# Row sums of a 64 MiB array: three row blocks of 32, 48 and 48 in place of two of 80 and 48, and the early stores issued one load earlier

## The chip, the core and the metric

The kernel runs on one core of a Trainium2 chip. Its time is the device time of one execution in microseconds (us). The kernel before was run three times: 160.71, 161.05 and 161.06 us, so its median is 161.05 us. One further execution was taken with the profiler; it took 160.77 us, of which the trace covers a span of 159.4 us.

## The reference: what is computed

The input `x` is float32 of shape 32 x 512 x 1024. The output is the sum over the last axis, float32 of shape 32 x 512:

```python
def reference(x):
    return np.sum(x, axis=-1).astype(np.float32)
```

Seen flat, that is 16384 rows of 1024 numbers (4 KiB each), 67.1 MB to read, and 16384 sums (64 KiB) to write. There are two float32 numbers of reading for each addition, so the work is almost only the reading.

## The kernel before, in words

**Layout.** The 128 partitions of the on-chip memory share the 16384 rows, 128 rows to each. Rows are dealt out in two blocks. Block a holds the first 128 x 80 rows: partition p gets 80 neighbouring rows, so where partition p+1 starts lies 80 rows (320 KiB) after partition p in the chip's main memory. Block z holds the other 128 x 48 rows in the same manner, with 48 rows (192 KiB) from one partition to the next. This distance is called the pitch below. The output of a block is cut likewise: partition p writes 80, or 48, neighbouring sums.

**Loads.** A block is read in groups of 16 rows a partition (G), so that one full load moves 128 x 64 KiB = 8.39 MB. Block a makes five groups (b = 0 to 4) and block z two (b = 5, 6); the last 16 rows of block z are read in smaller pieces of 9, 4 and 2 rows (`CUTS`: piece0, piece1, piece2) and the very last row in two parts of 544 and 480 numbers (tail0, tail1). Group 0 is read as one row (`first`) and 15 rows. Groups rotate through three buffers xt0 to xt2 (BUFS). All DMAs are issued by SyncE (SP in the profile), in the order of the list `loads` (line 134). From the fourth group on each load first waits until VectorE has finished the group that used the buffer before (line 133). The first two loads are moved ahead of the start barrier (lines 158 to 177).

**Sums.** VectorE sums each group with one reduction (lines 56 to 63) into `res_a` or `res_z`. In group 6 it takes 9 rows and ScalarE the other 7, one activation with accumulation for each (lines 65 to 71). The pieces are shared out in the same manner (lines 113 to 123); the two parts of the last row are summed by VectorE with a fused add and reduction (lines 73 to 79, called in lines 125 and 128), the second of which yields the last sum.

**Stores.** Behind all loads, SP waits for tail0's landing (line 135), for VectorE and ScalarE to have finished groups 0 to 6 (lines 136 and 137), and then issues two early stores: the 80 sums a partition of block a and the first 32 of block z (lines 138 and 139). Then it waits for all of VectorE's and ScalarE's work (lines 140 and 141) and issues the last store, 16 sums a partition (line 142). At the end it waits for both early stores and clears the semaphores (lines 145 and 146), and waits for the last store (line 147).

The order of instructions is written out by hand: each engine runs its own list in program order, and waits are on semaphores. A DMA adds 16 to its semaphore when it has landed, one for each of the 16 DMA engines that carry it.

Of the kernel before, what the change touches and what calls it, by code (L numbers as in the profile page):

```python
# [6 lines left out]
COPY = mybir.ActivationFunctionType.Copy  # L7
X = mybir.AxisListType.X

BODY = 80  # L10
Z = 48
G = 16
BUFS = 3
ACT_ROWS = 7
# [5 lines left out]
def row_sums(nc, x: bass.AP, out: bass.AP):  # L20
    P = nc.NUM_PARTITIONS
    x_flat = x.flatten_outer_dims()
    R, D = x_flat.shape
    C = R // P
    assert R % P == 0 and C == BODY + Z and BODY % G == 0 and Z % G == 0
    out_flat = out.rearrange("a (b c) -> (a b c)", c=1)

    def block(r0, n):
        x_b = x_flat[r0 : r0 + P * n].rearrange("(p c) d -> p (c d)", p=P)
        out_b = out_flat[r0 : r0 + P * n].rearrange("(p c) -> p c", p=P)  # L30
        return x_b, out_b

    x_a, out_a = block(0, BODY)
    x_z, out_z = block(P * BODY, Z)

    def sbuf(name, n):
        return nc.alloc_sbuf_tensor(name, [P, n], F32)

    xt = [sbuf(f"xt{i}", G * D) for i in range(BUFS)]
    tail = sbuf("tail", D + 16)  # L40
    pairs = [sbuf(f"pairs{i}", D // 2) for i in range(3)]
    res_a = sbuf("res_a", BODY)
    res_z = sbuf("res_z", Z)
    z0 = Z - G

    names = [f"slot{i}" for i in range(BUFS)] + ["first", "piece0", "piece1", "piece2", "tail0"]
    names += ["tail1", "vec", "act", "early_store", "store"]
    sems = {n: nc.alloc_semaphore(n) for n in names}
    slots = [sems[f"slot{i}"] for i in range(BUFS)]
    vec, act = sems["vec"], sems["act"]  # L50
    numbers = [s.num for s in sems.values()]
    assert numbers == list(range(numbers[0], numbers[0] + len(numbers)))

    count = {"vec": 0, "act": 0}

    def rows_dve(t, j, n, res, c):
        nc.vector.tensor_reduce(  # L57
            out=res[:, c : c + n],
            in_=t[:, j * D : (j + n) * D].rearrange("p (j d) -> p j d", d=D),
            axis=X,  # L60
            op=ADD,
        ).then_inc(vec, 1)
        count["vec"] += 1

    def rows_act(t, j, n, res, c):
        for i in range(n):
            v = t[:, (j + i) * D : (j + i + 1) * D]
            nc.scalar.activation(  # L68
                out=v, in_=v, func=COPY, accum_out=res[:, c + i : c + i + 1]
            ).then_inc(act, 1)  # L70
            count["act"] += 1

    def pairs_dve(t, a, b, acc, pairs):
        h = (a + b) // 2
        nc.vector.tensor_tensor_reduce(  # L75
            out=pairs[:, 0 : h - a], in0=t[:, a:h], in1=t[:, h:b], scale=1.0, scalar=0.0,
            op0=ADD, op1=ADD, accum_out=acc,
        ).then_inc(vec, 1)
        count["vec"] += 1

    n_bufs = (C - G) // G


    freed = {}
    loads = []
    for b in range(n_bufs):
        x_b, c = (x_a, b * G) if b * G < BODY else (x_z, b * G - BODY)
        parts = [(0, G, slots[b % BUFS])] if b else [(0, 1, sems["first"]), (1, G, slots[0])]
        for i, j, s in parts:
            loads.append((b, xt[b % BUFS][:, i * D : j * D], x_b[:, (c + i) * D : (c + j) * D], s))  # L90
    last = xt[n_bufs % BUFS]
    for k, (i, j) in enumerate(zip(CUTS, CUTS[1:])):
        loads.append((n_bufs, last[:, i * D : j * D], x_z[:, (z0 + i) * D : (z0 + j) * D], sems[f"piece{k}"]))
    for k, (i, j, gap) in enumerate(((0, CUT, 0), (CUT, D, 16))):
        e = (Z - 1) * D
        loads.append((0, tail[:, i + gap : j + gap], x_z[:, e + i : e + j], sems[f"tail{k}"]))


    nc.vector.memset(tail[:, CUT + 15 : CUT + 16], 0.0).then_inc(vec, 1)  # L99
    count["vec"] += 1  # L100
    nc.vector.wait_ge(sems["first"], 16)
    for b in range(n_bufs):
        a = ACT_ROWS if b == n_bufs - 1 else 0
        nc.vector.wait_ge(slots[b % BUFS], 16 * (b // BUFS + 1))
        res, c = (res_a, b * G) if b * G < BODY else (res_z, b * G - BODY)
        rows_dve(xt[b % BUFS], 0, G - a, res, c)
        freed[b] = count["vec"]
        if a:
            nc.scalar.wait_ge(slots[b % BUFS], 16 * (b // BUFS + 1))
            rows_act(xt[b % BUFS], G - a, a, res, c + G - a)  # L110
    body_vec, body_act = count["vec"], count["act"]

    for k in range(2):
        i, j = CUTS[k], CUTS[k + 1]
        h = (j - i) // 2
        nc.vector.wait_ge(sems[f"piece{k}"], 16)
        rows_dve(last, i, h, res_z, z0 + i)
        nc.scalar.wait_ge(sems[f"piece{k}"], 16)
        rows_act(last, i + h, j - i - h, res_z, z0 + i + h)
    nc.scalar.wait_ge(sems["piece2"], 16)  # L120
    rows_act(last, 14, 1, res_z, z0 + 14)
    nc.vector.wait_ge(sems["piece2"], 16)
    pairs_dve(last, 13 * D, 14 * D, res_z[:, z0 + 13 : z0 + 14], pairs[2])
    nc.vector.wait_ge(sems["tail0"], 16)
    pairs_dve(tail, 0, CUT, tail[:, CUT + 14 : CUT + 15], pairs[0])
    nc.vector.wait_ge(sems["tail1"], 16)
    nc.vector.wait_ge(vec, count["vec"])
    pairs_dve(tail, CUT + 14, D + 16, res_z[:, Z - 1 : Z], pairs[1])


    for b, dst, src, s in loads:
        if b >= BUFS:
            nc.sync.wait_ge(vec, freed[b - BUFS])
        nc.sync.dma_start(out=dst, in_=src).then_inc(s, 16)  # L134
    nc.sync.wait_ge(sems["tail0"], 16)
    nc.sync.wait_ge(vec, body_vec)
    nc.sync.wait_ge(act, body_act)
    nc.sync.dma_start(out=out_a, in_=res_a[:, :]).then_inc(sems["early_store"], 16)
    nc.sync.dma_start(out=out_z[:, 0:z0], in_=res_z[:, 0:z0]).then_inc(sems["early_store"], 16)
    nc.sync.wait_ge(vec, count["vec"])  # L140
    nc.sync.wait_ge(act, count["act"])
    nc.sync.dma_start(out=out_z[:, z0:Z], in_=res_z[:, z0:Z]).then_inc(sems["store"], 16)


    nc.sync.wait_ge(sems["early_store"], 32)
    nc.sync.sem_clear(range(numbers[0], sems["store"].num))
    nc.sync.wait_ge(sems["store"], 16).then_inc(sems["store"], -16)


def kernel(tc: tile.TileContext, x: bass.AP, out: bass.AP):  # L150
    tc.close()
    tc.compile()  # L152
    nc = tc.nc
    row_sums(nc, x, out)

    sp = mybir.EngineType.SP
    fn = nc.m.functions[0]
    entry, body = None, None  # L160
    for blk in fn.blocks:
        ops = [i for i in blk.instructions if i.engine == sp]
        if entry is None:
            entry = blk
        elif any(i.opcode == "DMACopy" for i in ops):
            body = blk
            break
    code = list(body.instructions)
    loads = [i for i in code if i.engine == sp and i.opcode == "DMACopy"][:EARLY]
    for load in loads:  # L170
        assert not load.sync_info.on_wait
        code.remove(load)
    body.instructions = code
    code = list(entry.instructions)
    at = next(k for k, i in enumerate(code) if i.engine == sp and i.opcode == "Drain")
    code[at:at] = loads
    entry.instructions = code
# [29 lines left out]
```

## Time and profile before

| what | value |
|---|---|
| median of three runs | 161.05 us (160.71 to 161.06) |
| the profiled execution | 160.77 us |
| its traced span | 159.4 us |
| VectorE (DVE) busy | 121.4 us, 76% of the span |
| ScalarE (ACT) busy | 17.2 us, 11% |
| DMA | 98.0% of 16 engines' span, 67.18 MB, mean 421 GB/s |
| one full reduction, 16 rows | 17.22 us |
| DMA packets | 2304 |

The profile has several views. The chain of waits follows the work that ended last backwards, and prints it in order of time. The timeline lists instructions by start, with the idle time of the engine before them and what ended it. The stretches table gives each engine's busy time, the DMA share and GB/s between two times. Below all this the trace keeps a record of every DMA packet (start, duration, bytes) and of every increment of a semaphore by a landed DMA; a packet of a full load is one partition's 64 KiB. Records are counted to a stretch by their start, so a DMA share above 1 in a short stretch means that long packets started in it. "SPq" in the views is the queue of instructions of SyncE: its DMA issues count as no engine's busy time.

### The profile page before, as it was taken

Reading aid. Unit: us, or ns where it says so; the run is one execution under the profiler, and the core shown is the slowest. Engines: PE = TensorE matmul, PEld = TensorE weight load, DVE = VectorE, ACT = ScalarE, POOL = GpSimd, SP = SyncE. Lnnn points to the kernel's source line nnn. Section 1 sums busy time; section 2 is a strip of 40 time slices with the busy share of each in tenths; the row PEclk is TensorE's granted clock in tenths of the full one; section 3 lists DMA queues with packets and bytes.
Section 4 is the critical chain, followed back from the end, with each engine's and each line's share of the span. In section 5 each row is a group of like instructions: output and inputs, shape, how many; then the busy total and the mean of one; then the engine's idle time right before and its main releaser. Section 6 shows DMA issues by size and latency. Waiting matters only on the chain.

```text
span 159.4 us, 108 instructions
## 1 busy us (share of the span) xinstructions
DVE 121.4 (76%) x16; ACT 17.2 (11%) x31; POOL 0.2 (0%) x4
## 2 busy tenths in 40 slices
DVE  0000049998699968999599994999949999499785
ACT  3000000000000000000000000000000000394694
POOL 0000000000000000000000000000000000000000
DMA  9969996996997989969969969969969989699994
GB/s 378 493 293 447 493 526 263 526 493 296 526 460 329 526 378 411 526 296 493 526 263 526 526 263 526 510 280 526 493 296 526 427 362 526 296 444 444 395 405 138
DMA packets 2304, 67.18 MB, mean 421 GB/s; under 512 B 640, under 2 KB 768, under 8 KB 1024
## 3 DMA queue, kind: packets, MB, share of 16 engines
q1 hardware_dynamic: 2304, 67.18, 98.0%
HBM read 67.11 MB, written 0.07 MB: 421 GB/s over the span
## 4 chain that ended last, share of the span: by engine, by line
DMA 75%; DVE 22%; SPq 1%; issue 0%
DMA xt<-in_x_dram 50%; DMA tail<-in_x_dram 25%; DVE res_a L57 22%; SPq L134 1%; DVE pairs L75 0%; DVE res_z L75 0%
## 5 line engine op out<-in xcount | busy, mean ns | idle before, releaser
L57 DVE TENSOR_REDUCE res_a<-xt 128x16 f32<-128x16384 f32 x5 | 86.1, 17220 | 28.4 <-DMA xt<-in_x_dram 28.4
L57 DVE TENSOR_REDUCE res_z<-xt 128x16 f32<-128x16384 f32 (+3 forms) x4 | 33.7, 8420 | 5.9 <-DMA xt<-in_x_dram 5.9
L68 ACT ACTIVATE xt<-xt 128x1024 f32<-128x1024 f32 x15 | 15.6, 1043 | 138.3 <-DMA xt<-in_x_dram 138.3
L68 ACT ACTIVATION_READ_ACCUMULATOR xt<-xt 128x1 f32 x15 | 2.8, 186 | 0.0
L99 DVE MEMSET tail<- 128x1 f32 x1 | 0.1, 59 | 2.0 <-PEq L152 2.0
L68 ACT ACT_TABLE_LOAD x1 | 1.3, 1283 | 1.9 <-PEq L152 1.9
L75 DVE CUSTOM_DVE_ANT_0 pairs<-tail 128x272 f32<-128x272 f32 (+1 forms) x2 | 0.9, 427 | 0.1
L75 DVE CUSTOM_DVE_ANT_0 pairs<-xt 128x512 f32<-128x512 f32 x1 | 0.7, 693 | 0.2 <-DMA xt<-in_x_dram 0.2
L75 DVE DVE_READ_ACCUMULATOR2_ANT res_z<- 128x1 f32 x2 | 0.2, 84 | 0.0
L191 POOL MEMSET const-bfloat16-1.0<- 128x1 bf16 x1 | 0.1, 102 | 0.0
L191 POOL MEMSET const-uint8-127<- 128x1 uint8 x1 | 0.1, 102 | 0.0
L191 POOL MEMSET const-float32-1.0<- 128x1 f32 x1 | 0.1, 99 | 0.0
L191 POOL MEMSET const-float32-0.0<- 128x1 f32 x1 | 0.1, 98 | 0.2 <-issue 0.2
L75 DVE DVE_READ_ACCUMULATOR2_ANT tail<- 128x1 f32 x1 | 0.1, 83 | 0.0
## 6 DMA issues: line engine op xcount, KB each, us to landing
xt<-in_x_dram SPq DMA_DIRECT2D x1, 7680.0 KB, 21.4
xt<-in_x_dram SPq DMA_DIRECT2D x1, 4608.0 KB, 32.3
xt<-in_x_dram SPq DMA_DIRECT2D x1, 2048.0 KB, 36.9
xt<-in_x_dram SPq DMA_DIRECT2D x1, 1024.0 KB, 38.9
xt<-in_x_dram SPq DMA_DIRECT2D x1, 512.0 KB, 3.7
tail<-in_x_dram SPq DMA_DIRECT2D x1, 272.0 KB, 39.1
tail<-in_x_dram SPq DMA_DIRECT2D x1, 240.0 KB, 39.2
xt<-in_x_dram SPq DMA_DIRECT2D x6, 40.8
```

The lines of the kernel that those rows point to most:

```text
L57: nc.vector.tensor_reduce(out=res[:, c : c + n], in_=t[:, j * D : (j + n) * D].rearrange("p (j d) -> p j d", d=D), axis=X, op=ADD,).then_i ...
L68: nc.scalar.activation(out=v, in_=v, func=COPY, accum_out=res[:, c + i : c + i + 1]).then_inc(act, 1)
L75: nc.vector.tensor_tensor_reduce(out=pairs[:, 0 : h - a], in0=t[:, a:h], in1=t[:, h:b], scale=1.0, scalar=0.0, op0=ADD, op1=ADD, accum_out ...
L99: nc.vector.memset(tail[:, CUT + 15 : CUT + 16], 0.0).then_inc(vec, 1)
L134: nc.sync.dma_start(out=dst, in_=src).then_inc(s, 16)
L191: nc = _bacc.Bacc("TRN2", target_bir_lowering=False, num_devices=1)
```

## The change

Two things are changed. The rows are dealt out in three blocks of 32, 48 and 48 rows a partition. Groups, buffers, pieces and reductions keep their sizes and their order: the first block makes two groups of 16 rows, the second three, the third two and the same pieces. The pitch is 128 KiB in the first block and 192 KiB in the other two. The results of a block lie in a tensor of their own (`sums[k]`), so there are three early stores, of 32, 48 and 32 sums a partition.

The early stores' first wait is for piece2, the load ahead of tail0, and no longer for tail0; the other two waits stay. The three stores follow one another with no further wait. The wait ahead of the clearing of the semaphores counts to 48 and no longer to 32.

```diff
-BODY = 80
-Z = 48
+BLOCKS = (32, 48, 48)
...
-    x_a, out_a = block(0, BODY)
-    x_z, out_z = block(P * BODY, Z)
+    xs, outs = [], []
+    r0 = 0
+    for n in BLOCKS:
+        xs.append(x_flat[r0 : r0 + P * n].rearrange("(p c) d -> p (c d)", p=P))
+        outs.append(out_flat[r0 : r0 + P * n].rearrange("(p c) -> p c", p=P))
+        r0 += P * n
...
-    res_a = sbuf("res_a", BODY)
-    res_z = sbuf("res_z", Z)
+    sums = [sbuf(f"res{i}", n) for i, n in enumerate(BLOCKS)]
+    x_z, res_z = xs[-1], sums[-1]
+    Z = BLOCKS[-1]
...
+    groups = []
+    for k, n in enumerate(BLOCKS):
+        c = 0
+        end = n - G if k == len(BLOCKS) - 1 else n
+        while c < end:
+            m = min(G, end - c)
+            groups.append((k, c, m))
+            c += m
+    n_bufs = len(groups)
...
-    nc.sync.wait_ge(sems["tail0"], 16)
+    nc.sync.wait_ge(sems["piece2"], 16)
     nc.sync.wait_ge(vec, body_vec)
     nc.sync.wait_ge(act, body_act)
-    nc.sync.dma_start(out=out_a, in_=res_a[:, :]).then_inc(sems["early_store"], 16)
-    nc.sync.dma_start(out=out_z[:, 0:z0], in_=res_z[:, 0:z0]).then_inc(sems["early_store"], 16)
+    for k, n in enumerate(BLOCKS):
+        end = z0 if k == len(BLOCKS) - 1 else n
+        nc.sync.dma_start(out=outs[k][:, 0:end], in_=sums[k][:, 0:end]).then_inc(sems["early_store"], 16)
     nc.sync.wait_ge(vec, count["vec"])
     nc.sync.wait_ge(act, count["act"])
-    nc.sync.dma_start(out=out_z[:, z0:Z], in_=res_z[:, z0:Z]).then_inc(sems["store"], 16)
-    nc.sync.wait_ge(sems["early_store"], 32)
+    nc.sync.dma_start(out=outs[-1][:, z0:Z], in_=res_z[:, z0:Z]).then_inc(sems["store"], 16)
+    nc.sync.wait_ge(sems["early_store"], 16 * len(BLOCKS))
```

## The prediction

> **What bounds the kernel now.** I read the chain of waits first, for what ends last; then the stretches table, for how near the load stream is to a limit; then the timeline of the end; and last the packet records, for the start. The chain:
>
> ```profile
> 21 pieces in order of time: start us, us, what
> 1.84 0.06 issue
> 1.90 39.31 DMA xt<-in_x_dram
> 41.21 0.02 issue
> 41.24 17.23 DVE res_a L57
> ...
> 118.34 39.16 DMA tail<-in_x_dram
> 157.50 0.06 issue
> 157.55 0.41 DVE pairs L75
> 157.97 0.01 DVE res_z L75
> ```
>
> The reader is to see that the chain is made of loads, and of reductions only where one frees a buffer for a load; even there the load waits in a full queue (39 us from issue to landing). After the last load only 0.47 us of VectorE follow. So the kernel ends when the DMA queue has drained, plus a short tail. The stretches say how hard the queue runs (columns: stretch, length, DVE, ACT, POOL, clock, DMA share, GB/s):
>
> ```profile
> 0.00:1.00 1.00, 0.00 (x0) 0.00 (x0) 0.20 (x4) 1.00 0.00 0
> ...
> 21.90:41.20 19.30, 17.22 (x1) 0.00 (x0) 0.00 (x0) 1.00 1.00 435
> 41.20:99.30 58.10, 51.68 (x4) 0.00 (x0) 0.00 (x0) 1.00 1.00 433
> ```
>
> The reader is to see a share of 1.00: no engine pauses between packets, so only a packet's own duration could shorten the stream. That is 2.418 us by the median for 64 KiB, in block a (pitch 320 KiB) and in block z (192 KiB) alike; the six groups of such packets average 2.4195 to 2.4229 us. VectorE has slack: it idles 2.1 us ahead of each full reduction. The tail:
>
> ```profile
> 156.29 0.69 DVE L75 CUSTOM_DVE_ANT_0 pairs<-xt 128x512 f32<-128x512 f32 x1 [0.21 <-DMA xt<-in_x_dram]
> ...
> 156.95 0.35 SPq L138 DMA_DIRECT2D out_dram<-res_a  x1
> ...
> 157.34 0.43 SPq L139 DMA_DIRECT2D out_dram<-res_z  x1
> 157.55 0.41 DVE L75 CUSTOM_DVE_ANT_0 pairs<-tail 128x241 f32<-128x241 f32 x1
> 157.89 0.08 DVE L75 DVE_READ_ACCUMULATOR2_ANT res_z<- 128x1 f32 x1
> 158.00 0.33 SPq L142 DMA_DIRECT2D out_dram<-res_z  x1
> ```
>
> The reader is to see that piece2 has landed by 156.29 (VectorE starts on it), tail0 by 156.95 (the first early store starts), and that SP is free again at 157.77, 0.23 us before the last sum lets it issue the last store at 158.00. That store lands 1.41 us later, at 159.41, where the span ends. Both early stores have landed by 158.87.
>
> **The change, part by part.**
>
> *Unchanged work.* Reductions, activations, pieces and load sizes are the same, seven groups in the same order with the same waits: 0. Where block borders move, only addresses change.
>
> *Blocks 1 and 2 (48 rows).* Their pitch, 192 KiB, is in the trace: block z streams at 2.418 us a packet. Cost 0.
>
> *Block 0 (32 rows, pitch 128 KiB).* This pitch is in no row. It concerns two groups, 16 packets an engine one after the other, 2 x 19.34 = 38.7 us. Nearest rows: 2.418 us at 320 and at 192 KiB, which gives 0. Slow bound: the longest full packet in the trace, 2.472 us, for all 16: 16 x 0.054 = +0.86 us. Below 2.418 us nothing is seen among 768 packets of either pitch, and the share is 1.00; the engines themselves set this floor, so no gain here. I take 0, because two pitches so different give the same number.
>
> The Trainium skill has a rule that speaks against this part. "DMA: Bandwidth & Descriptors", section "Latency and other measured facts", says that main-memory copies slow down when the row pitch is a large power of two: 207 GB/s at 512 KiB against a full 214, 164 at 2 MiB. The new pitch is a power of two and the old ones are not, but it is smaller than any pitch listed; by the 512 KiB figure block 0 would take 3.4% longer, an estimate from that page of +1.3 us, while by the trace's rows it takes no longer. No row of this trace shows such a slowing.
>
> *The start.* The first DMA is one row a partition, 128 packets of 4 KiB. From 1.0 to 2.6 us 33 of them take over 175 ns where the rest take 159; they lose 7.9 us together, 0.5 us an engine. The slowest engine loses more: undisturbed, group 0 would take 1.0 (to the first packet) + 8 x 0.159 + 8 x 2.267 + 0.44 (landing) = 20.85 us, and it lands at 21.86. The last engine's lag then stays to the end, since all run at one pace (the landings of groups 0 and 1 are both spread over 0.61 us). The cause of these slow packets is not visible. If it is the pitch, the new pitch can win at most 1.0 us, or lose as much again; if it is the first touch of the memory or the ramp of the queue, 0. Later first touches (block z, from 96 us on) are undisturbed at another pitch too. I take 0, and keep -1.0 and +1.0 for the range.
>
> *The early stores.* They start at 156.29 and no longer at 156.95: the other two waits have long been met (ScalarE's group 6 ends at 145.4, VectorE's at 147.7), so piece2 decides. Behind the waiting instruction SP holds only the three stores and the last one; no load is queued behind it. Issues follow one another at 0.39 us (stores 1 and 2 above) and 0.48 us (the loads issued from 116.9 on): starts 156.29, 156.68, 157.16, and SP is free at 157.59, 0.41 us ahead of 158.00. The third issue (0.43 us) is hidden behind the last row's landing and sum; if that cover were gone, the last store would move by the 0.43 us. The stores land some 1.53 us after issue, the third at 158.7, ahead of 159.41, so the wait for 48 and the clearing stay hidden. Moving the stores ahead gains nothing by itself: nobody waits for them but the clearing.
>
> *What the earlier issues disturb.* Issuing a DMA while packets stream makes those packets longer: in the four groups with one issue beside them, mostly 8 to 16 ns; with the five issues between 116.5 and 118.3 us, 28 to 54 ns. Before, the stores were issued when the slowest engine was in tail1; now one or two are issued while it is still in tail0 and tail1. That is 1 to 3 times 10 to 16 ns on the engine that ends last: 0.01 to 0.05 us, taken as +0.03 us. The stores' packets themselves (11 to 29 ns each) are queued behind the tail's on every engine: before, the first store's packets started 0.85 us after its issue, which now gives 157.14, just after the last tail packet has ended at 157.06. So they take nothing from the loads.
>
> **The sum.** 160.77 (profiled execution) + 0 + 0 + 0.03 = 160.80 us. That execution lies 0.28 us under the median of the runs, 161.05, from where the sum is 161.08. All four times average 160.90, which makes 160.93. I forecast 161.0 us, in the middle of the last two: no change that can be told. About 0.3%, 0.48 us, is what a measurement of this kernel can tell from none.
>
> **Rivals.**
>
> *A, slower: the new pitch.* At 128 KiB the 16 engines' addresses may fall on fewer places of the memory at once, and block 0's packets grow. Place: groups 0 and 1. Price: 16 packets an engine times the growth; it decides from 30 ns a packet on (16 x 0.030 = 0.48 us), and at the slow bound it is +0.86 us, 161.9. It can't hide, since each load is behind the other in one queue. For it: all start points of partitions become multiples of 128 KiB, and the start has shown packets of up to 758 ns. Against it: identical durations at 192 and 320 KiB.
>
> *B, faster: the start.* The slow first packets come from the old pitch and go with it. The slowest engine gains 0.5 to 1.0 us and keeps it to the end: 160.0 to 160.5 us. For it: the lag is real and lies on the bound. Against it: the slow packets stop after 2.6 us while the pitch stays, which looks like a start, not like a pitch. The mirror case, a slower start, belongs to A's sign, up to 162.0.
>
> *C, slower by SP's queue.* Were the three issues to take over 1.71 us (156.29 to 158.00), 0.57 us each, the last store would slip. The longest issue in the trace is 0.45 us, so I give it next to nothing; at 0.7 us each it is +0.4, 161.4.
>
> *D, the change doesn't do what it says.* If another wait decided, the stores would start late as before, at 156.95, and the third issue would end at 158.25 and the last store start at 158.29 where it started at 158.00: +0.3 us, within no change.
>
> **How the numbers follow.** My forecast with D, and what of C stays under 0.48 us: 0.58. A with the slower start: 0.24, and C's rest 0.01, so slower 0.25. B: 0.17. The runs vary by 0.35 us, so the forecast alone covers 160.6 to 161.5. To leave out no more than 2 in 10 the range takes in most of B (from 160.2) and A to its slow bounds (162.0). What it leaves out is the extremes: both gains of the start at once with a good run, and a pitch that costs more than any packet shown.
>
> **What would show it.** Right: the median of block 0's 64 KiB packets stays at 2.418 us; group 1 is reduced some 19.3 us after group 0; the first early store is issued near 156.3 us (moved by the start's lag), SP idles about 0.4 us ahead of the last store, and that store lands 1.4 us after its issue. Wrong by A: reductions in the first 41 us start later, with a DMA share still near 1.00 but under 434 GB/s. Wrong by B: the first reduction starts well before 21.96 us, and every later mark is earlier by as much. Wrong by C: SP never idles between the third early store and the last. What would make all of it wrong is an end that moves though the start, the pace and the tail don't.

## The result and the profile after

The changed kernel took 160.62 us by the median of 22 runs (160.44 to 161.07); the kernel before took 160.83 us by the median of 22 runs beside them (160.63 to 161.18). The ratio is 0.9987, with a 95% interval of 0.9981 to 0.9993. So it is faster by 0.13%, 0.21 us, which is real by the interval and lies within the 0.3% that the prediction called no change. The profiled execution took 160.68 us with a span of 159.3 us; before these were 160.77 and 159.4.

The chain of waits of the kernel after (columns: start, length, what) is the same chain:

```profile
1.91 39.17 DMA xt<-in_x_dram
41.08 0.02 issue
41.10 17.23 DVE res L56
...
118.25 39.19 DMA tail<-in_x_dram
157.44 0.02 issue
157.46 0.41 DVE pairs L74
157.87 0.01 DVE res L74
```

The reader is to see that the first piece is shorter by 0.14 us (39.17 against 39.31), and that the later marks are early too: 41.10 against 41.24, and 157.46 against 157.55. What this one execution gained, it gained before group 1. VectorE's first reduction shows it, first before, then after:

```profile
21.96 17.22 DVE L57 TENSOR_REDUCE res_a<-xt 128x16 f32<-128x16384 f32 x1 [19.92 <-DMA xt<-in_x_dram]
```

```profile
21.83 17.22 DVE L56 TENSOR_REDUCE res<-xt 128x16 f32<-128x16384 f32 x1 [19.79 <-DMA xt<-in_x_dram]
```

The stretches of the kernel after, same columns as before:

```profile
0.00:1.00 1.00, 0.00 (x0) 0.00 (x0) 0.20 (x4) 1.00 0.00 0
1.00:2.00 1.00, 0.02 (x1) 0.09 (x1) 0.00 (x0) 1.00 1.02 270
...
21.90:41.20 19.30, 17.24 (x2) 0.00 (x0) 0.00 (x0) 1.00 1.01 435
41.20:99.30 58.10, 51.70 (x4) 0.00 (x0) 0.00 (x0) 1.00 1.00 433
```

The reader is to see that the stream runs at 435 and 433 GB/s as before, also from 21.9 to 41.2 us, where group 1 is read at the new pitch. In the second microsecond 270 GB/s start where it was 205, by this line of the kernel before:

```profile
1.00:2.00 1.00, 0.02 (x1) 0.09 (x1) 0.00 (x0) 1.00 0.96 205
```

The end, on the timeline:

```profile
156.16 1.30 SPq L144 DMA_DIRECT2D out_dram<-res  x3
...
156.17 0.69 DVE L74 CUSTOM_DVE_ANT_0 pairs<-xt 128x512 f32<-128x512 f32 x1 [0.20 <-DMA xt<-in_x_dram]
...
157.46 0.41 DVE L74 CUSTOM_DVE_ANT_0 pairs<-tail 128x241 f32<-128x241 f32 x1 [0.17 <-DMA tail<-in_x_dram]
157.80 0.08 DVE L74 DVE_READ_ACCUMULATOR2_ANT res<- 128x1 f32 x1
157.91 0.33 SPq L147 DMA_DIRECT2D out_dram<-res  x1
```

The reader is to see three early stores issued in one run of 1.30 us from piece2's landing on. They end at 157.46, so SP idles 0.45 us before it can issue the last store at 157.91. VectorE now waits 0.17 us for tail1.

Three marks split every span of this study without a rest: group 0's landing (the last of its 16 engines), from there to piece2's landing, and from there to the end. Before: 21.858 + 134.408 + 3.174 = 159.440 us. After: 21.727 + 134.417 + 3.198 = 159.342 us. So in these two executions the start gave -0.131, the stream +0.009 and the tail +0.024. They are one execution each; how far starts of one kernel differ is shown below.

### The profile page after: what moved, and what is told of

It is laid out like the page before. It is cut to its first block, busy times and chain, and to the rows that moved or that the text cites. A ratio compares the mean times of both kernels' runs of the same rounds, so it can differ in the third digit from the quotient of the medians.

```text
span 159.3 us, 109 instructions
## 1 busy us (share of the span) xinstructions
DVE 121.4 (76%) x16; ACT 17.2 (11%) x31; POOL 0.2 (0%) x4
## 4 chain that ended last, share of the span: by engine, by line
DMA 75%; DVE 22%; SPq 1%; issue 0%
DMA xt<-in_x_dram 50%; DMA tail<-in_x_dram 25%; DVE res L56 22%; SPq L138 1%; DVE pairs L74 0%; DVE res L74 0%
## 5 line engine op out<-in xcount | busy, mean ns | idle before, releaser
L56 DVE TENSOR_REDUCE res<-xt 128x16 f32<-128x16384 f32 (+3 forms) x9 | 119.8, 13309 | 34.1 <-DMA xt<-in_x_dram 34.1
```

The source lines that it names most:

```text
L56: nc.vector.tensor_reduce(out=res[:, c : c + n], in_=t[:, j * D : (j + n) * D].rearrange("p (j d) -> p j d", d=D), axis=X, op=ADD,).then_i ...
```

## The experiments

Theory P: the gain comes from the start, because the first block's pitch is smaller. Rivals: theory S, it comes from issuing the stores earlier; theory N, neither, and sets of runs differ by as much. Each kernel below is the changed kernel with the edit shown. Ratios are to the kernel before, run beside it.

| run | blocks, early stores | ratio (95% interval) | group 0 lands | stream | tail |
|---|---|---|---|---|---|
| e1_blocks_only | 32, 48, 48; three at tail0 | 1.0018 (1.0009 to 1.0026) | 21.826 | 134.449 | 3.559 |
| e2_stores_only | 80, 48; two at piece2 | 0.9996 (0.9987 to 1.0004) | 22.020 | 134.408 | 3.179 |
| e3_48_32_48 | 48, 32, 48; three at piece2 | 0.9993 (0.9981 to 1.0004) | 21.795 | 134.403 | 3.201 |
| e4_16_64_48 | 16, 64, 48; three at piece2 | 1.0019 (1.0010 to 1.0028) | 22.160 | 134.594 | 3.193 |
| e5_32_96 | 32, 96; two at piece2 | 0.9996 (0.9987 to 1.0005) | 21.870 | 134.423 | 3.179 |
| e6_128 | 128; one at piece2 | 1.0008 (1.0000 to 1.0017) | 21.899 | 134.721 | 3.181 |
| e7_after_again | 32, 48, 48; three at piece2 | 0.9992 (0.9983 to 1.0000) | 21.910 | 134.402 | 3.194 |
| e8_one_first_load | the same, one first load | 0.9994 (0.9984 to 1.0005) | 22.314 | 134.398 | 3.173 |
| e12_32_96_late | 32, 96; two at tail0 | 0.9992 (0.9983 to 1.0001) | 21.789 | 134.408 | 3.183 |

The last three columns are of one profiled execution each, in us; the ratios are of 11 or 12 runs.

### The blocks with the stores as late as before

```diff
-    nc.sync.wait_ge(sems["piece2"], 16)
+    nc.sync.wait_ge(sems["tail0"], 16)
     nc.sync.wait_ge(vec, body_vec)
```

> The three blocks of 32, 48 and 48 rows, but the early stores wait for tail0 as in the kernel before. Theory P (the gain of 0.13% comes from the start: the first block's pitch of 128 KiB makes the first loads' slow packets fewer, so the first reduction starts near 21.8 us and every later mark is earlier by as much): ratio 0.998 to 0.999, the first early store near 156.8 us. Theory S (the gain comes from issuing the early stores at piece2): ratio 1.000, at worst 1.002 since the third issue now ends after the last sum.

It is slower: 161.22 us against 160.98, ratio 1.0018. Theory P's mark (0.998 to 0.999, a first reduction near 21.8 us) isn't met, the reduction starts at 21.93; theory S's "at worst 1.002" is. On its timeline the last sum is ready and the store isn't issued:

```profile
156.96 1.30 SPq L144 DMA_DIRECT2D out_dram<-res  x3
...
157.90 0.08 DVE L74 DVE_READ_ACCUMULATOR2_ANT res<- 128x1 f32 x1
158.35 0.38 SPq L147 DMA_DIRECT2D out_dram<-res  x1
```

The reader is to see that the three issues last from 156.96 to 158.26, past VectorE's end at 157.98; the last store starts at 158.35 and no longer at 158.00. The tail is 3.559 us, 0.385 more than before. So the earlier wait is what pays for the third store: without it the third issue stands on the path. The median rose by 0.24 us and not by 0.385, which would leave some -0.14 us to the blocks; the interval of the ratio is 0.14 us wide to either side, so this doesn't show a gain.

### The earlier stores alone

```diff
-BLOCKS = (32, 48, 48)
+BLOCKS = (80, 48)
```

> Blocks of 80 and 48 rows as before, the early stores issued at piece2. Theory P: ratio 1.000, with some 0.03 to 0.06 us lost between the landing of piece2 and that of tail1, because the stores are issued beside the last row's packets. Theory S: ratio 0.998 to 0.999 with the first reduction near 21.95 us.

160.91 against 160.98 us, 0.9996, with an interval on both sides of 1. Its tail is 3.179 us, 0.005 more than before, and the first reduction starts at 22.12 us. Theory S's mark (0.998 to 0.999) isn't met, and the tail isn't shorter; the ratio's interval alone wouldn't exclude 0.999. Theory P's loss between the landings of piece2 and tail1 (0.03 to 0.06 us) came out at 0.02.

### Another order, and a still smaller first pitch

```diff
-BLOCKS = (32, 48, 48)
+BLOCKS = (48, 32, 48)   # e3
+BLOCKS = (16, 64, 48)   # e4
```

> The changed kernel with blocks of 48, 32 and 48 rows: pitches of 192, 128 and 192 KiB, the 128 KiB one no longer at the start. Theory P, if a smaller pitch at the start is what helps: the ratio lies between, 0.9985 to 1.000, and the first reduction between 21.8 and 21.95 us; if only a first pitch that is a power of two helps, 1.000. Theory S: 0.9987 as the changed kernel. Rival A of the prediction (128 KiB slows a stretch): groups 3 and 4 would have packets above 2.43 us on average.

> The changed kernel with blocks of 16, 64 and 48 rows: the first pitch is 64 KiB, so the first group is one stretch of memory without holes, and the second block has 256 KiB. Theory P with a smaller pitch as the cause: ratio 0.997 to 0.9985, first reduction at or before 21.8 us. Theory S: 0.9987 with no change of the start. Should 256 KiB slow the middle block, its four groups' packets average above 2.43 us, and 0.01 us more a packet would cost 0.32 us.

e3, with 192 KiB at the start: 0.9993, with a first reduction at 21.89 us; this lies in theory P's band and its interval takes in 1, so it decides nothing. Its packets in groups 3 and 4, now at 128 KiB, average 2.4202 and 2.4196 us: no slowing. e4 is a miss for theory P with "smaller is better": 161.34 us, slower by 0.19%. VectorE's starts in e4:

```profile
22.26 17.22 DVE L56 TENSOR_REDUCE res<-xt 128x16 f32<-128x16384 f32 x1 [20.22 <-DMA xt<-in_x_dram]
41.75 17.22 DVE L56 TENSOR_REDUCE res<-xt 128x16 f32<-128x16384 f32 x1 [2.27 <-DMA xt<-in_x_dram]
61.08 17.22 DVE L56 TENSOR_REDUCE res<-xt 128x16 f32<-128x16384 f32 x1 [2.11 <-DMA xt<-in_x_dram]
```

The reader is to see a first start 0.3 us later than before (21.96), and a step of 19.49 us to the next, where it was 19.28 before and where the second step takes 19.33. In group 1, the first at 256 KiB, single packets took up to 2.886 us; in groups 2 to 4, at the same pitch, the average is 2.4181 to 2.4189. So 256 KiB costs something in its first group here and nothing later. In e4's profile the stream takes 0.19 us more than before, so only the rest of the loss can lie at the start with its 64 KiB.

### Two blocks, one block, and the changed kernel again

```diff
-BLOCKS = (32, 48, 48)
+BLOCKS = (32, 96)       # e5
+BLOCKS = (128,)         # e6
```

> The changed kernel with two blocks of 32 and 96 rows: the first pitch stays 128 KiB, the second is 384 KiB, and there are two early stores at piece2 in place of three. Theory P (the first pitch sets the start): as the changed kernel and a little better for the store left out, ratio 0.998 to 0.9995. Theory N (start and pitch have nothing to do with each other; the gain of the changed kernel lies within what sets of runs differ by): ratio 1.000 within 0.0007.

> The changed kernel with one block of 128 rows: a pitch of 512 KiB for all loads, one early store of 112 sums a partition. It tells how much a large power of two costs at all. Rival A of the prediction: packets of all groups above 2.43 us; the figure of 207 against 214 GB/s that a page gives for this pitch would make the stream 3.4% longer, an estimate of some 166 us. By the trace's packets at 128, 192 and 256 KiB, all 2.418 to 2.420 us: ratio 0.999 to 1.001, with the rest depending on the start.

> The changed kernel itself once more, beside new runs of the kernel before. If the gain is real: ratio 0.998 to 0.9993 again, with a first reduction near 21.8 us. Theory N: the ratio may come out at 1.000.

e5 came out just above theory P's band, at 0.9996; it tells neither P nor N. e7, the changed kernel itself, came out at 0.9992: the gain showed again, smaller, with an interval that ends at 1.0000. Its first reduction starts at 22.01 us, later than in either profile shown above and than the expected 21.8, so one execution's start says little: with the same first block, the starts in these profiles differ by 0.2 to 0.3 us.

e6 has the whole array at 512 KiB and loses 0.08%, with an interval that begins at 1.0000. Its averages by group from group 1 on, from the packet records, are 2.454, 2.430, 2.422 and then 2.418 to 2.421 us: slow at first, then as any other.

### One first load

```diff
-        parts = [(0, m, slots[b % BUFS])] if b else [(0, 1, sems["first"]), (1, m, slots[0])]
+        parts = [(0, m, slots[b % BUFS])]
...
-    nc.vector.wait_ge(sems["first"], 16)
```

> The changed kernel with group 0 as one load of 16 rows and no row of its own ahead, so that there are no 4 KiB packets at the start, and VectorE's wait for that row goes too. If the 4 KiB packets make the last engine's lag: the lag, and the spread of group 0's landings over 0.6 us, shrink, the first reduction starts near 21 to 21.5 us and the ratio is 0.996 to 0.998. If the ramp of the queue makes it, whatever the packet: the ratio is 0.999 or above, since the longer first load also takes longer to prepare.

0.9994: the expectation for a ramp of the queue, not that for the 4 KiB packets. The slow start moves into the 64 KiB packets: in group 0 they average 2.526 us, up to 3.566, and an engine loses 8 x 0.108 = 0.86 us on average.

### More starts in one execution

In these three kernels (e10 and e11 with `BLOCKS` of 80, 48 and of 128) each full load from group 1 on is issued only when the one before has landed, so that the queue runs empty ("drained") ahead of each:

```diff
-    for b, dst, src, s in loads:
+    for k, (b, dst, src, s) in enumerate(loads):
+        if 2 <= k <= n_bufs:
+            q = b - 1
+            nc.sync.wait_ge(slots[q % BUFS], 16 * (q // BUFS + 1))
```

> The changed kernel with the queue emptied between groups: each full load from group 1 on is issued only when the one before it has landed, so there are six more starts to look at in one execution. Each should cost some 1.3 us (0.85 to the first packet, 0.44 for landing) plus what the new start loses. If the start's loss is the ramp of a queue whatever came before, groups 1 to 6 lose some 0.5 to 1 us each as group 0 does, and the time is near 173 us; if it is a first touch, they lose next to nothing and the time is near 169 us. Theory P: groups 0 and 1 (128 KiB) lose less than groups 2 to 6 (192 KiB).

> The same with blocks of 80 and 48 rows. Theory P: groups 0 to 4 (320 KiB) take longer from first packet to landing than the changed kernel's groups 0 and 1, by 0.1 to 0.3 us each, and the time is 0.3 to 1 us above the other drained kernel. Theory N: the two agree within 0.2 us.

> The same with one block of 128 rows, a pitch of 512 KiB. In the undrained one the packets of groups 1 and 2 averaged 2.454 and 2.430 us and then 2.418: if engines that start together get in each other's way at this pitch until they have drifted apart, every drained group shows it, some 0.2 to 0.3 us each, and the time is 1 to 2 us above the other drained kernels. If it was the first touch alone, groups 3 to 6 are as fast as at the other pitches.

Their medians are 175.65, 176.12 and 179.26 us, of 4 runs each; the intervals of the first two ratios, 1.0905 to 1.0935 and 1.0930 to 1.0960, just overlap. All are above what was expected of a ramp (near 173 us), and far from a first touch (near 169). VectorE's starts, first of e9 (blocks of 32, 48, 48), then of e10 (80, 48), then of e11 (128):

```profile
21.93 17.22 DVE L56 TENSOR_REDUCE res<-xt 128x16 f32<-128x16384 f32 x1 [19.89 <-DMA xt<-in_x_dram]
43.70 17.22 DVE L56 TENSOR_REDUCE res<-xt 128x16 f32<-128x16384 f32 x1 [4.55 <-DMA xt<-in_x_dram]
65.42 17.22 DVE L56 TENSOR_REDUCE res<-xt 128x16 f32<-128x16384 f32 x1 [4.50 <-DMA xt<-in_x_dram]
87.34 17.22 DVE L56 TENSOR_REDUCE res<-xt 128x16 f32<-128x16384 f32 x1 [4.70 <-DMA xt<-in_x_dram]
```

```profile
22.24 17.22 DVE L56 TENSOR_REDUCE res<-xt 128x16 f32<-128x16384 f32 x1 [20.20 <-DMA xt<-in_x_dram]
44.05 17.22 DVE L56 TENSOR_REDUCE res<-xt 128x16 f32<-128x16384 f32 x1 [4.58 <-DMA xt<-in_x_dram]
65.83 17.22 DVE L56 TENSOR_REDUCE res<-xt 128x16 f32<-128x16384 f32 x1 [4.56 <-DMA xt<-in_x_dram]
87.75 17.22 DVE L56 TENSOR_REDUCE res<-xt 128x16 f32<-128x16384 f32 x1 [4.70 <-DMA xt<-in_x_dram]
```

```profile
45.05 17.22 DVE L56 TENSOR_REDUCE res<-xt 128x16 f32<-128x16384 f32 x1 [5.08 <-DMA xt<-in_x_dram]
67.42 17.22 DVE L56 TENSOR_REDUCE res<-xt 128x16 f32<-128x16384 f32 x1 [5.16 <-DMA xt<-in_x_dram]
89.79 17.22 DVE L56 TENSOR_REDUCE res<-xt 128x16 f32<-128x16384 f32 x1 [5.14 <-DMA xt<-in_x_dram]
```

The reader is to see the steps between starts: 21.77 us to e9's group 1 (128 KiB), then 21.72 and 21.92 (192 KiB); 21.81, 21.78 and 21.92 in e10 (320 KiB); 22.37 twice in e11, where a step of the undrained kernels is some 19.34. By the records, from issue to landing, e9's group at 128 KiB takes 21.83 us, e10's four groups at 320 KiB take 21.77 to 21.90, and the seven groups at 192 KiB 21.70 to 21.93. Of that, 0.96 us go to the first packet, 19.34 to the stream and 0.31 to 0.36 to landing (from the last packet's end); the rest, 1.1 to 1.3 us, is lost by the engine that ends last, every time. So the start's loss belongs to every start of an empty queue, not to a first touch of the memory, and for 64 KiB packets it is the same at 128, 192 and 320 KiB. At 512 KiB it is larger, by 0.5 us on average (issue to landing 22.13 to 22.44 us), about twice what was expected. Theory P's mark, 0.1 to 0.3 us between groups of e9 and of e10, isn't met. The whole times do differ its way, by 0.47 us, of 4 runs each; the two profiles' spans differ by as much (174.35 and 174.82), and 0.3 us of it is there before group 1 is issued (at 21.84 and 22.16 us), that is in group 0 with its 4 KiB row.

### The pitch alone

```diff
-BLOCKS = (32, 48, 48)
+BLOCKS = (32, 96)
...
-    nc.sync.wait_ge(sems["piece2"], 16)
+    nc.sync.wait_ge(sems["tail0"], 16)
```

> Blocks of 32 and 96 rows with two early stores that wait for tail0: the tail as in the kernel before, and only the pitch differs (128 KiB at the start). Theory P: ratio 0.9985 to 0.9995. Theory N: 1.000 within 0.0007.

160.85 against 160.94 us, 0.9992 (0.9983 to 1.0001): in theory P's band, with theory N not excluded. Two early stores at tail0 are the tail of the kernel before, so here the addresses, and with them the split of the stores, are all that differs.

## Why the prediction was right

The forecast was 161.0 us and no change that can be told; measured were 160.62 us and -0.13%. Of the 0.38 us between, 0.17 are in the base, since the kernel before had 160.83 us in the runs beside it, and 0.21 are the gain. By its steps:

- **Unchanged work and blocks 1 and 2: 0.** Right. From group 0's landing to piece2's, the stream took 134.40 to 134.45 us in the nine profiles with pitches of 128, 192, 320 and 384 KiB.
- **Block 0's pitch: 0, slow bound +0.86 us.** Right. At 128 KiB the packets' median is 2.418 or 2.420 us wherever that block stood. Their average in group 1 was 2.4220 us in the kernel after and 2.4197 to 2.4206 in e1, e5, e7 and e12. Single packets of the kernel after took up to 2.509 us there, above the slow bound of 2.472, but its stream lost no more than 0.01 us. Rival A didn't happen.
- **The rule on row pitch.** The Trainium skill's page "DMA: Bandwidth & Descriptors", section "Latency and other measured facts", has 207 against 214 GB/s at 512 KiB, for copies between tensors in main memory. Here, in loads to on-chip memory, that pitch cost 0.08% of the time in e6 and not 3.4%, and only near a start. The page infers, unverified by its own word, that streams in lock step get in each other's way. Packets that are slow only near a start would fit that, but no run here shows the cause.
- **The early stores: hidden, nothing gained by themselves.** Right. The three issues ran from 156.16 to 157.46 us, 0.45 us ahead of the last store (predicted 0.41), and that store landed 1.40 us after its issue. The price given for a lost cover holds too: the prediction's case D puts the last store at 158.29 and the loss at +0.3 us; with the wait put back, e1 shows 158.35, +0.24 us in the median and +0.385 us in the tail. The issues of one queue thus do come onto the path, though not by the slow issues of rival C (they took 1.30 us and not 1.71), and only the earlier wait keeps them off it.
- **What the earlier issues disturb: +0.03 us.** Measured +0.024 in the tail after, +0.020 in e7, +0.005 in e2 with two stores. The size is partly luck: tail1 landed 0.06 us later behind piece2 than before (1.295 against 1.232 us), and 0.03 of it didn't reach the last sum because VectorE started on it 0.02 us after that landing, where it had taken 0.06 before. As foreseen, the stores' own packets took nothing from the loads: the first started at 157.00, after the last load packet's end at 156.96.
- **The start: 0, bounds -1.0 and +1.0.** If any term was mis-sized it is this one, by 0.1 to 0.2 us. The median's -0.21 us less the tail's +0.02 leaves -0.23 us for it in the first set of runs. The four sets that begin with 32 rows as two loads and have a covered tail are all below 1: 0.9987, 0.9992, 0.9996 and 0.9992. But e2, with 80 rows first, has 0.9996 as well, so the ratios don't tell 32 rows from 80. First reductions start at 21.83, 22.01, 21.93, 21.97, 21.89 and 21.93 us in the six profiles with a first block of 32 rows that is loaded in two parts (after, e7, e1, e5, e12, e9), and at 21.96, 22.12 and 22.24 in the three with 80 rows (before, e2, e10): averages 21.93 and 22.11, in ranges that overlap. That speaks for the start and for about 0.1 to 0.2 us, but doesn't show it; it is far from rival B's 0.5.
- **What the slow first packets are.** The prediction left the cause open between the pitch and the ramp of the queue, and took 0. Drained groups lose as much at 128, 192 and 320 KiB, which speaks for the ramp. Theory P's fewer slow packets aren't there: 4 KiB packets over 175 ns number 24 to 38 in the six profiles with 32 rows, 20 to 33 in the three with 80, and they lose 9.2 and 9.5 us in all on average. What differs is when the last engine lands the one-row load: at 3.48 to 3.78 us with 32 rows, at 3.74 to 4.04 with 80. From there to group 0's landing all nine take 18.08 to 18.25 us. Two small slips of the prediction: block z's packets start at 98.25 us and not at 96, and group 0's landing took 0.36 us from the last packet's end and not 0.44, so that the slowest engine's loss was 1.09 us and not 1.0.

**What stays open.** Whether the start is shorter by the change at all, and why. The smallness of the pitch doesn't explain it (64 KiB gains nothing, and starts at 22.26 us), nor does it show in drained groups with 64 KiB packets. What is left is the first load's 4 KiB packets, whose addresses the change moves; that wasn't tried by itself, and e8, without them, can't be told from e7. With starts that vary by 0.2 to 0.3 us from one execution to the next, a single profile can't tell it. No version here beats the changed kernel by more than the intervals.

## What to carry to other kernels

When the DMA queue never pauses, split the time into the first landing, the stream and the tail: then each edit can be looked for in its place. Here edits of stores acted on the tail alone (up to 0.385 us), and the stream stayed within 0.05 us in nine profiles; pitches of 256 and 512 KiB alone moved it, by 0.19 and 0.31 us. A store added near the end costs nothing only as long as all issues, some 0.4 us each on one queue, end before the last result is ready; count them, and put their first wait early enough. Compare many runs, not two profiles, when the question is 0.1%.

## What the runs showed of the hardware that was not expected

An empty DMA queue lost 1.1 to 1.3 us on its slowest engine at each of the twelve starts in e9 and e10, beside 0.96 us to the first packet and 0.31 to 0.36 us for landing: six more starts in one execution made 14.8 us (175.65 against e7's 160.88 for the same kernel undrained). The first start of an execution lost about as much, 1.0 to 1.4 us with 4 KiB packets in the nine profiles above. A pitch of 512 KiB added 0.5 us on average to each such start; undrained (e6), packets of groups 1 and 2 averaged 2.454 and 2.430 us, and those from the fourth group on 2.418 to 2.421.
